# A hybrid decoder layer on one core: one of seven activation tiles moved by 448 bytes within the partition

## The chip, the cores and the metric

The kernel runs on one core of a Trainium2 chip. The time is that of the device for one execution, in microseconds (us). The profile is one execution taken by the hardware profiler; its rows give times in us from the first instruction of the span.

## What is computed

One decoder layer for 512 positions of width 2048, in float32: a combined input projection, eight heads of block-sparse attention beside a Mamba-2 scan, an output projection, and a convolutional gated feed-forward. The change concerns the feed-forward, whose two large products are most of the work of the second half:

```
h = rms_norm(x, norm2_w)
u = causal_dwconv(h @ w_up, ffn_conv_w, ffn_conv_b)      # 2048 -> 2 x 5632
u_gate, u_val = jnp.split(u, 2, axis=-1)
return x + (jax.nn.silu(u_gate) * u_val) @ w_down        # 5632 -> 2048
```

## The kernel before

**Parts.** Ahead of the feed-forward, the projections and the attention's products run through `acc_tile` and `sm_tile` (their instructions stand under line L183, the line of a helper that records them). The feed-forward, from `start_up` and `step_slot` on, is a list of products (`items`) that is run in the order in which it is written; no scheduler changes it.

**High and low parts.** [...]

**Seven products.** The feed-forward's matrix products are made by a Strassen-like scheme: 2 x 2 blocks with seven products P1 to P7 instead of eight. Each product has a fixed kind of activations, which is a combination of blocks, held in a tile of its own: P5 uses `cmb0`, P7 `cmb1`, P1 `cmb2`, P6 `cmb3`, P2 `cmb4`, P3 `cmb5` (K22) and P4 `cmb6` (KT4). A group is one block column of the weights with its seven products. There are 44 groups of the up-projection with eight chunks of 128 rows, and 24 of the down-projection in three passes, with seven, eight and seven chunks. A product of eight chunks is 24 matmuls of 128 x 256, one of seven chunks 21. In the running order the groups are laced: P5 of a group, P3 of the group before, P1, P4 of the group before, P6, P2, P7. In a row of the profile all products but P2 write a tile `x`, and P2 writes `y`; the activation tiles all read `cmb`, so a product is told by its place in the order.

```
    for gi in range(len(groups) + 1):
        for d, x in ((0, "P5"), (1, "P3"), (0, "P1"), (1, "P4"), (0, "P6"), (0, "P2"), (0, "P7")):
            put(gi - d, x)
```

The matmuls of a product are these (`h`, `l` the weights' parts, stationary; `bk` the tile of the kind, moving):

```
                pe.matmul(out, w, bk[:, 0, q, :], start=fresh and q == 0, stop=False, skip_group_check=True)
                pe.matmul(out, w, bk[:, 1, q, :], start=False, stop=False, skip_group_check=True)
            for q in part:
                pe.matmul(out, l[:, q * 128:(q + 1) * 128], bk[:, 0, q, :], start=False, stop=q == n - 1,
```

In chunk q the moving operand starts 1,024 bytes times q into its half of the tile, and the stationary one 512 bytes times q into its tile; both steps are whole numbers of 512, so the difference of their places by 512 is the same in every chunk.

**Places.** A tile takes the same bytes in each of the 128 partitions. The pool `lp` (left side, named `w2`) holds the weights' tiles and `cmb5` and `cmb6`, which are made in `x_split` for the up-projection and in `b_split` for the down passes; the pool `cmb` on the right side holds `cmb0` to `cmb4`. At the left end lies a scratch for DMA descriptors, 16,384 bytes, and everything of the left side stands behind it. The built program of before, and that of the change, have these places (first byte in the partition, and that number's rest by 512):

```
tile                          before                      rest  after                       rest
descriptor scratch            0 to 16383                        0 to 1023
hi2 (three buffers)           55840, 59936, 64032           32  40480, 44576, 48672           32
lo2 (two buffers)             68128, 72224                  32  52768, 56864                  32
cmb5 (P3)                     76320                         32  60960                         32
space                         -                                 77344 to 77791
cmb6 (P4)                     92704                         32  77792                        480
cmb0 (P5), cmb1 (P7)          147424, 163808               480  147424, 163808               480
cmb2 (P1), cmb3 (P6)          180192, 196576               480  180192, 196576               480
cmb4 (P2)                     212960                       480  212960                       480
earlier: A0..A15, B0..B15     46624 to 112159               32  31264 to 96799                32
earlier: hi (three buffers)   33952, 36064, 38176  160,224,288  18592, 20704, 22816  160,224,288
earlier: lo (three buffers)   40288, 42400, 44512  352,416,480  24928, 27040, 29152  352,416,480
attention: PTh, PTl           180192, 184288               480  180192, 184288               480
attention: vh, vl             188384, 192480               480  188384, 192480               480
```

**Order around the change.** TensorE's matmuls wait for ScalarE's `hi2` and VectorE's `lo2`, and the reuse of their results for VectorE and ScalarE, which add the products up. At the beginning of each down pass VectorE and ScalarE also split the seven kinds of the next pass (`b_split`, L1096 and L1097). Loads are issued by the queue of SyncE (SP).

Of the kernel before, what the change touches and what calls it, by code (L numbers as in the profile page):

```python
# [20 lines left out]
F32 = mybir.dt.float32  # L21
# [166 lines left out]
def body(ctx, tc, xT, wi, wz, wo, wu, wd0, wd1, wd2, pp, pf, outT, dbg={}):  # L188
    nc = tc.nc
# [672 lines left out]
    def cmb_tile(t):  # L862

        pool = p2["cmb"] if t < K22 else p2["cmbl"]
        return pool.tile([128, 2, 8, 256], F32R, name="cmb%d" % t)
# [104 lines left out]
    lp = ctx.enter_context(tc.tile_pool(name="w2", bufs=1, reuse_waits="tile"))  # L970
# [150 lines left out]
    def x_load(n):  # L1121
        if n < 4:
            x_ld.append(side_tile(box["pool"], [4, 256], "ld", 3))
            sy.dma_start(x_ld[n], xd[:, 4 * (n % 2):4 * (n % 2) + 4, n // 2, :])

    def x_split(n):
        t, h = (K22, KT4)[n // 2], n % 2
        if h == 0:
            up_kinds[t] = cmb_tile(t)
        o = up_kinds[t][:, :, 4 * h:4 * h + 4, :]  # L1130
        se.activation(o[:, 0], x_ld[n], AF.Copy)
        ve.tensor_tensor(o[:, 1], x_ld[n], o[:, 0].bitcast(F32), op=OP.subtract)
        x_load(n + 3)

    for n, slot in enumerate((2, 4, 5, 6)):
        at(slot, x_split, n)
# [135 lines left out]
    for k, (gi, x) in enumerate(items):  # L1272
# [8 lines left out]
        n = g["n"]  # L1281
# [36 lines left out]
```

## Time and profile before

| | us |
|---|---|
| three runs | 2113.61, 2114.42 (median), 2114.91 |
| the profiled execution's own time | 2114.84 |
| its span, first to last instruction | 2113.1 |
| TensorE busy in matmuls | 2073.9 |
| VectorE busy | 1583.5 |
| ScalarE busy | 988.3 |
| GpSimd busy | 207.9 |

The profiled execution lies 0.42 us above the median of the runs and 0.07 below the highest; 1.7 us of it lie outside the span. PE is TensorE, DVE VectorE, ACT ScalarE, POOL GpSimd, and PEld the loading of weights. Matmuls are pipelined, so the length of one in a row (0.28 us) is longer than the distance from its start to the next one's start; it is the starts that tell the pace.

### The profile page before, as it was taken

The numbers are of one execution on the slowest core, as the hardware profiler recorded it, in microseconds if no ns is written. First come the engines' busy times: TensorE is split into PE (matmuls) and PEld (weight loads), VectorE is DVE, ScalarE is ACT, GpSimd is POOL, SyncE is SP. The second block draws the span as 40 slices with busy tenths as digits, with TensorE's granted clock in tenths as the row PEclk, the third lists the DMA queues.
The fourth block names the chain that finished last, engine by engine and source line by source line (L and its number), as shares of the span: only waits on it lengthen the run. The fifth ranks groups of instructions, "written<-read, shape, count | busy, mean of one in ns | idle before, by whom it ended". The sixth has DMA issues, their size and how long they took to land.

```text
span 2113.1 us, 37694 instructions
## 1 busy us (share of the span) xinstructions
PE 2073.9 (98%) x15366; PEld 1949.7 (92%) x15366; DVE 1583.5 (75%) x2251; ACT 988.3 (47%) x1433; POOL 207.9 (10%) x107
## 2 busy tenths in 40 slices
PE   9999999999999998999999999999999899999999
PEld 7888887888888878999999999999999899899999
DVE  6545555345555558999999999999999977977976
ACT  5433435244344435555555555555555534534532
POOL 0020000000000001111110111011111111101110
PEclk9999999999999999999999999999999999999999
DMA  5233222332225535445444444454455667856763
GB/s 194 75 115 91 71 75 76 99 101 80 80 70 172 165 129 188 158 141 189 160 156 165 170 168 155 157 183 158 142 188 201 215 215 242 274 184 231 260 201 120
DMA packets 114396, 328.18 MB, mean 155 GB/s; under 512 B 10736, under 2 KB 35120, under 8 KB 111408
## 3 DMA queue, kind: packets, MB, share of 16 engines
q1 hardware_dynamic: 114224, 325.78, 45.5%
q8 instruction: 120, 1.97, 0.4%
q14 instruction: 52, 0.43, 0.1%
HBM read 283.77 MB, written 41.98 MB: 154 GB/s over the span
## 4 chain that ended last, share of the span: by engine, by line
PE 88%; DVE 7%; issue 2%; ACT 1%; DMA 1%; SPq 0%; DVEq 0%; POOL 0%; ACTq 0%; POOLq 0%
PE acc L183 29%; PE x L1289 16%; PE x L1286 16%; PE x L1287 16%; PE sm L183 4%; PE y L1289 3%; PE y L1287 3%; PE y L1286 3%; DVE lo L1050 2%; DVE cmb L1097 1%; DVE lo L183 1%; DVE acc L1151 0%; DVE s L1024 0%; DMA raw<-wi 0%; DVE s L1030 0%
## 5 line engine op out<-in xcount | busy, mean ns | idle before, releaser
L1287 PE MATMUL x<-cmb,hi 128*128 128x256 f32 x3168 | 755.0, 279 | 12.5 <-DVE cmb L1097 10.9
L1286 PE MATMUL x<-cmb,hi 128*128 128x256 f32 x3168 | 755.8, 279 | 11.5 <-ACT cP L1166 5.4
L1287 PEld LDWEIGHTS x<-cmb,hi 128*128 128x128 f32 x3168 | 599.3, 189 | 15.2 <-DVE cmb L1097 13.4
L1286 PEld LDWEIGHTS x<-cmb,hi 128*128 128x128 f32 x3168 | 598.7, 189 | 13.4 <-issue 7.5
L1289 PE MATMUL x<-cmb,lo 128*128 128x256 f32 x3168 | 434.3, 279 | 2.6 <-DVE lo L1050 2.6
L1289 PEld LDWEIGHTS x<-cmb,lo 128*128 128x128 f32 x3168 | 397.2, 189 | 3.6 <-DVE lo L1050 3.4
L183 DVE TENSOR_TENSOR lo<-raw,hi 128x512 fp32r<-128x512 f32 (+1 forms) x240 | 164.4, 691 | 243.0 <-ACT hi L183 228.5
L1041 ACT ACTIVATE hi<-s 128x1024 fp32r<-128x1024 f32 (+1 forms) x201 | 201.0, 1000 | 287.3 <-DVE s L1024 192.2
L1017 POOL TENSOR_TENSOR rawb<-rawa,rawb 128x1024 f32<-128x1024 f32 (+1 forms) x68 | 169.7, 2496 | 1308.1 <-DVE s L1024 1070.8
L183 PE MATMUL acc<-A,hi 128*128 128x512 f32 x704 | 281.5, 400 | 0.5 <-ACT hi L183 0.5
L183 PE MATMUL acc<-A,lo 128*128 128x512 f32 x704 | 277.9, 395 | 0.1
L183 PE MATMUL acc<-B,hi 128*128 128x512 f32 x704 | 276.8, 393 | 0.0
L183 ACT ACTIVATE hi<-raw 128x512 fp32r<-128x512 f32 (+1 forms) x240 | 149.6, 629 | 256.2 <-PE acc L183 220.3
L1050 DVE TENSOR_TENSOR lo<-s,hi 128x1024 fp32r<-128x1024 f32 (+1 forms) x201 | 238.6, 1187 | 18.8 <-issue 18.8
L1050 DVE TENSOR_TENSOR lo<-rawa,hi 128x1024 fp32r<-128x1024 f32 (+1 forms) x204 | 242.0, 1186 | 3.6 <-PE x L1289 3.6
L1041 ACT ACTIVATE hi<-rawa 128x1024 fp32r<-128x1024 f32 (+1 forms) x204 | 209.5, 1028 | 40.0 <-PE x L1287 39.9
L183 PEld LDWEIGHTS acc<-A,lo 128*128 128x128 f32 x704 | 132.1, 188 | 33.0 <-DVE lo L183 2.1
L183 PEld LDWEIGHTS acc<-A,hi 128*128 128x128 f32 x704 | 132.7, 188 | 29.5 <-ACT hi L183 1.8
L183 PEld LDWEIGHTS acc<-B,hi 128*128 128x128 f32 x704 | 132.5, 188 | 28.3
L1166 ACT ACTIVATE cP<-x 128x256 f32<-128x256 f32 x132 | 50.9, 385 | 214.0 <-PE x L1289 214.0
L183 PE MATMUL acc<-hi,A 128*128 128x256 f32 (+2 forms) x448 | 135.4, 302 | 0.7 <-DVE u L183 0.7
L183 PE MATMUL acc<-lo,A 128*128 128x256 f32 (+2 forms) x448 | 133.5, 298 | 0.0
(204 smaller groups left out, 2777.2 us busy)
## 6 DMA issues: line engine op xcount, KB each, us to landing
rawa<-wu SPq DMA_DIRECT2D x176, 512.0 KB, 3.6
raw<-wi SPq DMA_DIRECT2D x79, 512.0 KB, 3.6
rawa<-wd SPq DMA_DIRECT2D x64, 448.0 KB, 4.1
rawb<-wu SPq DMA_DIRECT2D x44, 512.0 KB, 4.5
gd<-gt SPq DMA_DIRECT2D x22, 1024.0 KB, 4.6
raw<-wo SPq DMA_DIRECT2D x32, 512.0 KB, 3.6
rawa<-wd SPq DMA_DIRECT2D x32, 512.0 KB, 4.4
ld<-gd SPq DMA_DIRECT2D x27, 512.0 KB, 6.4
```

Source lines behind the costliest of these rows:

```text
L183: return fn(out, *args, **kw)
L1017: po.tensor_tensor(r, raw[gi, "11"][:, :n], r, op=OP.subtract)
L1041: se.activation(h[:, :n], src[:, :n], AF.Copy)
L1050: ve.tensor_tensor(l[:, :n], src[:, :n], h[:, :n].bitcast(F32), op=OP.subtract)
L1097: ve.tensor_tensor(lo, ld[:, :m, :], hi.bitcast(F32), op=OP.subtract)
L1166: se.activation(g[x], X[:, 256:] if x == "P5" else X[:, :256], AF.Copy)
L1286: pe.matmul(out, w, bk[:, 0, q, :], start=fresh and q == 0, stop=False, skip_group_check=True)
L1287: pe.matmul(out, w, bk[:, 1, q, :], start=False, stop=False, skip_group_check=True)
L1289: pe.matmul(out, l[:, q * 128:(q + 1) * 128], bk[:, 0, q, :], start=False, stop=q == n - 1, skip_group_check=True)
```

## The change

A tile of 112 float32 numbers per partition, named `space`, is taken from the left pool between `cmb5` and `cmb6`; nothing reads or writes it. The scratch for DMA descriptors is made with 1,024 bytes instead of 16,384, so all tiles of the left side begin 15,360 bytes (30 times 512) further left; `cmb6` begins 14,912 bytes further left. Tiles of the right side stay. Each engine has the same instructions in the same order with the same waits; only line numbers behind the added lines are higher by 2.

```
@@ def x_split(n):
         t, h = (K22, KT4)[n // 2], n % 2
+        if n == 2:
+            lp.tile([128, 112], F32, name="space")
         if h == 0:
             up_kinds[t] = cmb_tile(t)
@@ def kernel(**inputs):
-    nc = _bacc.Bacc("TRN2", target_bir_lowering=False, num_devices=1)
+    nc = _bacc.Bacc("TRN2", target_bir_lowering=False, num_devices=1, dynamic_dma_scratch_size=1024)
```

## Rows read from the trace of the kernel before

**Rows 1.** The page: the span, busy time of each engine with its share of the span and its instructions, the DMA queues (packets, MB, share of 16 engines), and the shares by engine of the chain that ended last.

```profile
span 2113.1 us, 37694 instructions
...
PE 2073.9 (98%) x15366; PEld 1949.7 (92%) x15366; DVE 1583.5 (75%) x2251; ACT 988.3 (47%) x1433; POOL 207.9 (10%) x107
...
q1 hardware_dynamic: 114224, 325.78, 45.5%
q8 instruction: 120, 1.97, 0.4%
...
PE 88%; DVE 7%; issue 2%; ACT 1%; DMA 1%; SPq 0%; DVEq 0%; POOL 0%; ACTq 0%; POOLq 0%
```

**Rows 2.** Busy time by stretch of the span: from and to, length, busy time of PE, PEld, DVE, ACT and POOL (number of instructions), then the granted clock of TensorE, the busy share of the DMA engines and GB/s.

```profile
0.00:791.31 791.31, 782.68 (x4266) 664.45 (x4267) 415.14 (x795) 340.51 (x640) 36.32 (x38) 1.00 0.34 106
...
825.29:1649.45 824.16, 824.16 (x7154) 824.16 (x7153) 768.69 (x956) 430.53 (x555) 105.28 (x43) 1.00 0.46 165
1649.45:1707.62 58.17, 46.73 (x365) 44.66 (x364) 54.83 (x72) 30.56 (x36) 7.49 (x3) 0.97 0.73 250
1707.62:1801.99 94.37, 94.37 (x821) 94.37 (x820) 73.10 (x97) 37.12 (x41) 12.52 (x6) 1.00 0.70 231
1801.99:1838.08 36.09, 31.66 (x261) 30.35 (x259) 35.60 (x40) 23.34 (x25) 5.82 (x2) 1.00 0.88 301
1838.08:1967.66 129.58, 129.58 (x1128) 129.58 (x1126) 99.00 (x118) 52.26 (x53) 17.17 (x7) 1.00 0.62 211
1967.66:1994.26 26.60, 23.76 (x195) 22.77 (x193) 26.35 (x33) 15.85 (x19) 3.86 (x1) 1.00 0.85 291
1994.26:2100.68 106.42, 106.42 (x927) 106.42 (x925) 80.84 (x107) 39.81 (x44) 12.80 (x6) 1.00 0.53 177
```

**Rows 3.** TensorE's instructions in order of time in one group of the up-projection: start, length of the row, engine, line, operation, output and inputs, shape, how many. The products begin at 1400.49 (P3), 1403.35 (P1), 1406.09 (P4), 1408.95 (P6), 1411.69 (P2) and 1414.41 (P7).

```profile
1400.49 0.28 PE L1286 MATMUL x<-cmb,hi 128*128 128x256 f32 x1
...
1402.39 1.12 PE L1289 MATMUL x<-cmb,lo 128*128 128x256 f32 x8
1403.35 0.29 PE L1286 MATMUL x<-cmb,hi 128*128 128x256 f32 x1
1403.47 0.28 PE L1287 MATMUL x<-cmb,hi 128*128 128x256 f32 x1
1403.60 0.28 PE L1286 MATMUL x<-cmb,hi 128*128 128x256 f32 x1
1403.71 0.28 PE L1287 MATMUL x<-cmb,hi 128*128 128x256 f32 x1
...
1405.19 1.07 PE L1289 MATMUL x<-cmb,lo 128*128 128x256 f32 x8
1406.09 0.28 PE L1286 MATMUL x<-cmb,hi 128*128 128x256 f32 x1
...
1407.99 1.12 PE L1289 MATMUL x<-cmb,lo 128*128 128x256 f32 x8
1408.95 0.29 PE L1286 MATMUL x<-cmb,hi 128*128 128x256 f32 x1
...
1411.69 0.28 PE L1286 MATMUL y<-cmb,hi 128*128 128x256 f32 x1
...
1413.51 1.07 PE L1289 MATMUL y<-cmb,lo 128*128 128x256 f32 x8
1414.41 0.28 PE L1286 MATMUL x<-cmb,hi 128*128 128x256 f32 x1
```

**Rows 4.** The same view: the first matmul of P4 in the second group of the up-projection that runs P4, and in the 43rd, which is 41 groups later (the one before the first of these begins at 825.29).

```profile
844.65 0.28 PE L1286 MATMUL x<-cmb,hi 128*128 128x256 f32 x1
...
1638.41 0.28 PE L1286 MATMUL x<-cmb,hi 128*128 128x256 f32 x1
```

**Rows 5.** The same view in the last pass of the down-projection, seven chunks: the first matmul of P7, P5, P3, P1, P4 and P6.

```profile
1999.04 0.28 PE L1286 MATMUL x<-cmb,hi 128*128 128x256 f32 x1
...
2001.42 0.28 PE L1286 MATMUL x<-cmb,hi 128*128 128x256 f32 x1
...
2003.80 0.28 PE L1286 MATMUL x<-cmb,hi 128*128 128x256 f32 x1
...
2006.30 0.29 PE L1286 MATMUL x<-cmb,hi 128*128 128x256 f32 x1
...
2008.70 0.28 PE L1286 MATMUL x<-cmb,hi 128*128 128x256 f32 x1
...
2011.20 0.29 PE L1286 MATMUL x<-cmb,hi 128*128 128x256 f32 x1
```

**Rows 6.** What TensorE waited for from 1649.45 us to the end: the waiting line and its output, the releaser, us in total, times, the longest.

```profile
PE x L1287 <- DVE cmb L1097: 10.9, 11, 2.3
...
PE y L1287 <- DVE cmb L1097: 2.8, 3, 2.0
```

**Rows 7.** TensorE in order of time before the feed-forward, columns as in rows 3: a run of nine matmuls of attention with `PTh`, `PTl`, `vh` and `vl` and the one behind it, then a piece of a projection with 512 columns (moving A or B, stationary hi or lo).

```profile
268.25 0.28 PE L183 MATMUL sm<-PTh,vh 128*128 128x256 f32 x1
...
269.33 0.28 PE L183 MATMUL sm<-kh,qh 128*128 128x256 f32 x1
...
492.16 0.39 PE L183 MATMUL acc<-A,hi 128*128 128x512 f32 x1
...
493.54 0.39 PE L183 MATMUL acc<-A,hi 128*128 128x512 f32 x1
```

More of the change, by code (lines that the diff above doesn't have):

```diff
@@ L1127, in x_split @@
         t, h = (K22, KT4)[n // 2], n % 2
+        if n == 2:
+            lp.tile([128, 112], F32, name="space")
         if h == 0:
@@ L1306 @@
     from concourse.bass_utils import run_bass_kernel_spmd as _run
-    nc = _bacc.Bacc("TRN2", target_bir_lowering=False, num_devices=1)
+    nc = _bacc.Bacc("TRN2", target_bir_lowering=False, num_devices=1, dynamic_dma_scratch_size=1024)
     arrays = layout(**{k: _np.asarray(v) for k, v in inputs.items()})
```

## The prediction

> **What bounds the kernel now.** I read the head of the page first. TensorE is busy for 98% of the span, VectorE for 75%, and the chain that ended last lies on TensorE for 88% [rows 1]. Such shares are averages, so I cut the span where TensorE begins or ceases to wait [rows 2]. In four stretches its busy time equals the length of the stretch: 825.29 to 1649.45, 1707.62 to 1801.99, 1838.08 to 1967.66 and 1994.26 to 2100.68, together 824.16 + 94.37 + 129.58 + 106.42 = 1154.5 us. All four are made of the products P1 to P7, at a granted clock of 1.00. Between them lie the hand-overs to the next pass, where VectorE is busy nearly throughout (54.83 of 58.17 us, 35.60 of 36.09, 26.35 of 26.60) and TensorE waits, mostly for the split of a kind (L1097) [rows 2, 6]. So in the four stretches a nanosecond taken from a matmul comes off the end, and in the hand-overs it does not.
>
> Then I read the timeline of one group, product by product, since the change touches one product [rows 3]. A product ends where the next begins. P3 runs from 1400.49 to 1403.35, 2.86 us; P1 2.74; P4 2.86; P6 2.74; P2 2.72. Every product is the same 24 matmuls of 128 x 256. The rows of eight low-part matmuls show the pace itself: 1.12 us in P3 and P4, 1.07 in P1 and P2. One matmul is 0.28 long and seven more steps follow, so a step is (1.12 - 0.28)/7 = 0.120 us against (1.07 - 0.28)/7 = 0.113. No wait stands in these rows; the difference is in the matmuls. P3 and P4 stream `cmb5` and `cmb6`, and those are the two kinds whose first byte, counted by 512, is 32 like that of the weights; the other five stand at 480 (the table of places above).
>
> P1 and P6 are 0.02 us longer than P2, and the rows of P1 show where: its first three starts lie 0.12, 0.13 and 0.11 apart, from the fourth on 0.113 to 0.115. They are the two products that follow a slow one, and the slowness reaches a few matmuls into them.
>
> **What the change does, and its price.** The instructions, their order and their waits are the same; only places differ. Two things move.
>
> First, `cmb6` goes from 32 to 480 by 512, the place of the five fast kinds. P4 should then run like P2: 2.72 instead of 2.86, 0.14 us. P6 loses its slow start, 2.74 to 2.72, 0.02 us. That is 0.16 us of a group, whose length is now (1638.41 - 844.65)/41 = 19.36 us [rows 4]. In the down passes of seven chunks P7 and P5, from 1999.04 to 2003.80, take 2.38 each, P3 and P4 2.50, P1 2.40 [rows 5]: there the gain is 0.12 + 0.02 = 0.14. P3 stays slow and so does the start of P1.
>
> How often: there are 44 groups of up and 24 of down, 68 products P4, 52 of eight chunks and 16 of seven. Of them 43 lie in the first full stretch ((1638.41 - 825.29)/19.36 = 42, and one), 6 of seven in the second, 6 of eight in the third and 6 of seven in the fourth. That is 49 x 0.16 + 12 x 0.14 = 9.5 us. The other seven lie in hand-overs and at the end (3 x 0.16 + 4 x 0.14 = 1.0 us); where TensorE waits for VectorE's queue, arriving earlier only lengthens the wait. Bounds are nothing and all of that 1.0; I take 0.2, near nothing, because VectorE is busy for over 94% of each hand-over [rows 2].
>
> Does the faster TensorE run into VectorE? In the long stretch VectorE is busy 768.69 of 824.16 us [rows 2], so idle 55.5 us, 1.3 us a group, and the gain is 0.16. It stays hidden; without that cover, all of the 0.16 would be lost. ScalarE, at 430.53, and the DMA engines, at a share of 0.46 there and 0.70 in the second stretch, have more room.
>
> Second, the smaller scratch moves everything on the left by 15,360 bytes, which is 30 x 512. The distances among left tiles stay, so the 791 us before the products keep their time; distances from left to right tiles change by a multiple of 512. [...] I price this at nothing. The bound on the gain side is nothing too, since the five right-hand kinds already run at the fastest step seen; on the loss side it is the last rival.
>
> Sum: 9.5 + 0.2 = 9.7 us off the profiled execution's 2114.84 (span 2113.1 and 1.7 around it) gives 2105.1. The median of the runs, 2114.42, is 0.4 lower, so the forecast for the median is **2104.7 us**, 0.46% faster.
>
> **The rivals.** *The place, not the offset.* `cmb5` and `cmb6` are also the only two kinds that lie low in the partition, beside the weights; the other five lie above byte 147,000. If two tiles on one side disturb each other whatever their offset, P4 stays at 2.86 and the time at 2114.4. For it: before the products, moving and stationary operands both lie low at offsets that differ by 64 to 480, and the 512-column matmuls from 492.16 to 493.54 take (493.54 - 492.16)/6 = 0.230, or 0.115 for 256 columns, not 0.113 [rows 7]. Against it: attention's `PTh` and `vh` lie high, both at 480, and take (269.33 - 268.25)/9 = 0.120 [rows 7], exactly P4's step. Equal offsets give 0.120 on either side, unequal ones on one side give less. So the offset matters, and the side may matter a little.
>
> [...]
>
> *Half the gain.* If P4 comes to the 0.115 to 0.116 of low tiles at unequal offsets, it takes 24 x 0.1155 = 2.77 us and saves 0.09 a group of eight, 0.08 of seven: 49 x 0.09 + 12 x 0.08 = 5.4 us, 2109.0.
>
> *Slower.* The 15,360 bytes are a whole number of 1,024s, but not of 2,048s. If what counts is the distance by 2,048 or more, the five right-hand kinds get new distances from the weights, 106,944 instead of 91,584 for `cmb0`. A kind that lands badly costs what P4 costs now: 52 x 0.14 + 16 x 0.12 = 9.2 us. One such kind cancels the gain; from two on the kernel is slower, and as all five move alike it would be 5 x 9.2 - 9.7 = 36 us more, 2151. Against it: within a product the weights step by 512 and the activations by 1,024, so the distance passes through every multiple of 512, and P1's starts stay 0.113 to 0.115 apart over all eight chunks: (1405.19 - 1403.71)/13 = 0.114 [rows 3].
>
> **How the numbers follow.** Full gain 0.60, half gain 0.12, no change 0.21, slower 0.07. A change of under 0.2% (4.2 us) is about what a measurement of this kernel cannot tell from none, so faster is 0.60 + 0.12 = 0.72, same 0.21, slower 0.07. The likeliest case alone runs from 2103.4 (all 10.5 us, and 0.5 for the scatter of the runs) to 2106.5 (nothing kept in hand-overs, P4 only at 2.74, and 0.4 for the scatter). With half gain it holds 0.72, so the range must take in no change as well: 2103.4 to 2115.4.
>
> **What the next profile would show.** Right: rows of eight in P4 at 1.07, those of P3 still at 1.12; P4 2.72 and P6 2.72; a group of 19.20; the long stretch 43 x 0.16 = 6.9 us shorter, at 817.3, with VectorE's busy time unchanged; hand-overs as long as before; 791 us ahead of the products. Wrong: P4 still at 1.12 (the place), at 1.08 to 1.10 (half), rows of eight above 1.07 in P1, P2, P5, P6 or P7 (distance by more than 512), or waits of TensorE in the long stretch (VectorE after all).

## The result and the profile after

The changed kernel takes 2104.32 us (median of 4 runs, 2103.83 to 2104.76) where the kernel before, run beside it, takes 2114.66 (4 runs): a ratio of 0.995 with a 95% interval of 0.9932 to 0.9967. The forecast was 2104.7. The page of the profiled execution after, its span and the busy times of the engines, to be read against [rows 1]:

```profile
span 2102.1 us, 37694 instructions
...
PE 2061.9 (98%) x15366; PEld 1938.7 (92%) x15366; DVE 1582.6 (75%) x2251; ACT 988.3 (47%) x1433; POOL 207.9 (10%) x107
```

The span is 11.0 us shorter, and TensorE is busy 12.0 us less with the same 15366 matmuls; the busy times of VectorE, ScalarE and GpSimd are within 1 us of before. The next two views place the 11.0 us. Both give busy time by stretch, columns as in [rows 2]. Each stretch begins with the same product P5 in both kernels, so that lengths can be subtracted. First the kernel before, whose stretch ahead of these is in [rows 2]:

```profile
791.31:816.29 24.98, 17.70 (x132) 16.89 (x133) 17.70 (x24) 9.73 (x16) 6.68 (x3) 0.86 0.64 218
816.29:1649.45 833.16, 832.95 (x7227) 832.75 (x7226) 777.00 (x965) 438.00 (x564) 105.28 (x43) 1.00 0.46 165
1649.45:1717.29 67.84, 56.40 (x449) 54.33 (x448) 62.49 (x82) 33.13 (x39) 9.48 (x4) 0.97 0.71 239
1717.29:1801.99 84.70, 84.70 (x737) 84.70 (x736) 65.44 (x87) 34.55 (x38) 10.53 (x6) 1.00 0.71 238
1801.99:1846.26 44.27, 39.84 (x333) 38.53 (x331) 42.38 (x48) 25.57 (x27) 8.22 (x3) 1.00 0.78 267
1846.26:1962.42 116.16, 116.16 (x1011) 116.16 (x1009) 86.98 (x105) 45.22 (x46) 14.58 (x6) 1.00 0.62 213
1962.42:2001.42 39.00, 36.16 (x303) 35.16 (x301) 37.57 (x47) 22.58 (x26) 6.04 (x3) 1.00 0.78 264
2001.42:2086.12 84.70, 84.70 (x738) 84.70 (x736) 64.36 (x86) 32.34 (x36) 10.67 (x6) 1.00 0.60 199
2086.12:2113.10 26.98, 22.57 (x191) 22.03 (x189) 14.38 (x21) 6.67 (x8) 0.14 (x1) 1.00 0.18 63
```

The changed kernel, from its start:

```profile
0.00:790.29 790.29, 781.78 (x4266) 664.89 (x4267) 415.21 (x795) 340.34 (x640) 36.32 (x38) 1.00 0.33 106
790.29:815.17 24.88, 17.79 (x132) 17.19 (x133) 17.32 (x24) 10.09 (x17) 6.68 (x3) 0.86 0.66 231
815.17:1640.98 825.81, 825.81 (x7227) 825.81 (x7226) 776.29 (x964) 437.61 (x564) 105.07 (x43) 1.00 0.46 166
1640.98:1709.15 68.17, 55.41 (x449) 52.47 (x448) 62.75 (x82) 33.20 (x40) 9.66 (x4) 1.00 0.70 240
1709.15:1793.15 84.00, 84.00 (x737) 84.00 (x736) 65.39 (x87) 34.53 (x38) 10.55 (x6) 1.00 0.71 239
1793.15:1837.33 44.18, 39.76 (x332) 38.45 (x331) 42.38 (x48) 25.72 (x27) 8.19 (x3) 1.00 0.79 270
1837.33:1952.53 115.20, 115.20 (x1010) 115.20 (x1009) 86.98 (x105) 45.23 (x46) 14.56 (x7) 1.00 0.61 214
1952.53:1991.47 38.94, 35.84 (x302) 34.85 (x301) 37.57 (x47) 22.58 (x26) 6.04 (x3) 1.00 0.78 263
1991.47:2075.47 84.00, 84.00 (x737) 84.00 (x736) 64.35 (x86) 32.33 (x36) 10.65 (x6) 1.00 0.59 201
2075.47:2102.10 26.63, 22.34 (x191) 21.80 (x189) 14.39 (x21) 6.67 (x8) 0.14 (x1) 1.00 0.19 63
```

In the stretches in which TensorE never waits the gains are 7.35 (833.16 to 825.81), 0.70, 0.96 and 0.70 us. Of the 7.35, 6.88 are 43 groups by 0.16; the rest, 0.47, lies in one product P1 at the start of the stretch (2.75 us long now, 3.22 before), where TensorE waited 0.2 us for VectorE before and does not wait now. The hand-overs give -0.33, 0.09 and 0.06, and the end 0.35. Ahead of the feed-forward, whose start is at 790.29 instead of 791.31, lie 1.02, and 0.10 in its first waits. Together that is 11.0.

One group of the up-projection after, the rows of eight low-part matmuls of TensorE (those that read `lo`), columns as in [rows 3]. In order they belong to P4, P6, P2, P7, P5, P3 and P1:

```profile
1401.52 1.07 PE L1291 MATMUL x<-cmb,lo 128*128 128x256 f32 x8
1404.23 1.07 PE L1291 MATMUL x<-cmb,lo 128*128 128x256 f32 x8
1406.95 1.07 PE L1291 MATMUL y<-cmb,lo 128*128 128x256 f32 x8
1409.67 1.07 PE L1291 MATMUL x<-cmb,lo 128*128 128x256 f32 x8
1412.39 1.07 PE L1291 MATMUL x<-cmb,lo 128*128 128x256 f32 x8
1415.20 1.12 PE L1291 MATMUL x<-cmb,lo 128*128 128x256 f32 x8
1417.99 1.07 PE L1291 MATMUL x<-cmb,lo 128*128 128x256 f32 x8
```

Only P3 is left at 1.12, which is the pace of 0.120 us a matmul; P4 has come to 1.07, or 0.113. In starts of products: P4 2.720 us (2.861 before), P6 2.720 (2.739), P3 2.861 and P1 2.739 as before, the other three 2.720.

What TensorE waits for from 1640.98 us to the end, columns as in [rows 6]:

```profile
PE x L1289 <- DVE cmb L1097: 11.5, 12, 2.3
PE y L1289 <- DVE cmb L1097: 3.1, 3, 2.1
```

These are the waits of [rows 6], 10.9 and 2.8 us there, 0.9 us longer together: most of what TensorE gains inside a hand-over becomes wait.

### The profile page after: what moved, and what is told of

Same layout as the page of the kernel before. It is cut to its first block, busy times and chain, and to the rows that moved or that the text cites. A ratio compares the mean times of both kernels' runs of the same rounds, so it can differ in the third digit from the quotient of the medians.

```text
span 2102.1 us, 37694 instructions
## 1 busy us (share of the span) xinstructions
PE 2061.9 (98%) x15366; PEld 1938.7 (92%) x15366; DVE 1582.6 (75%) x2251; ACT 988.3 (47%) x1433; POOL 207.9 (10%) x107
## 4 chain that ended last, share of the span: by engine, by line
PE 90%; DVE 6%; DMA 2%; issue 1%; ACT 1%; SPq 0%; DVEq 0%; POOL 0%; ACTq 0%; POOLq 0%
PE acc L183 30%; PE x L1288 16%; PE x L1289 16%; PE x L1291 16%; PE sm L183 4%; PE y L1288 3%; PE y L1289 3%; PE y L1291 3%; DVE lo L1050 1%; DVE cmb L1097 1%; DMA rawa<-wd 1%; DMA ld<-gd 0%; DVE lo L183 0%; DVE acc L1153 0%; DVE s L1024 0%
```

## The experiments

Products below are medians in us over the up-projection, from the start of one product to the start of the next. "Distance" is the place of a kind's tile less that of the weights' tiles, by 512. Each experiment had its own runs of the kernel before beside it, with medians of 2113.2 to 2114.5. The kernels e4, e6, e7, e8 and e12 have one run each, the others four or more. Runs of one kernel lie 1 to 4 us apart (e1_both 11), so for those five the products say more than the time. No kernel leaves out any part of the computation.

| kernel | distance of `cmb5`, `cmb6` | P3 | P1 | P4 | P6 | P2, P7, P5 | us |
|---|---|---|---|---|---|---|---|
| before | 0, 0 | 2.861 | 2.739 | 2.861 | 2.739 | 2.720 | 2114.7 |
| the change | 0, 448 | 2.861 | 2.739 | 2.720 | 2.720 | 2.720 | 2104.3 |
| e5_mirror | 448, 0 | 2.720 | 2.720 | 2.861 | 2.739 | 2.720 | 2104.2 |
| e8_off_192_256 | 192, 256 | 2.720 | 2.720 | 2.861 | 2.739 | 2.720 | 2104.0 |
| e11_off_32_448 | 32, 448 | 2.803 | 2.738 | 2.720 | 2.720 | 2.720 | 2100.2 |
| e6_off_32_480 | 32, 480 | 2.803 | 2.738 | 2.834 | 2.753 | 2.720 | 2113.6 |
| e7_off_64_128 | 64, 128 | 2.830 | 2.727 | 2.849 | 2.827 | 2.826 | 2129.9 |
| e12_off_320_384 | 320, 384 | 2.830 | 2.727 | 2.849 | 2.827 | 2.827 | 2128.0 |
| e1_both | 448, 448 | 2.826 | 2.826 | 2.826 | 2.826 | 2.826 | 2130.7 |
| e4_right_equal | 0, 448; the others 0 | 2.880 | 2.880 | 2.739 | 2.861 | 2.880 | 2150.9 |

**Which part of the change it is.** e2_scratch_only takes the smaller scratch alone, e3_space_only the 448 bytes alone.

```
-    nc = _bacc.Bacc("TRN2", target_bir_lowering=False, num_devices=1)
+    nc = _bacc.Bacc("TRN2", target_bir_lowering=False, num_devices=1, dynamic_dma_scratch_size=1024)
```

> Only the smaller descriptor scratch: everything of the left side moves by 15,360 bytes, cmb6 stays at 32 by 512 like the weights. Offset theory: nothing changes, 2114.5, P3 and P4 at 2.86. If the scratch, or where the left side begins, carried part of the gain: between 2104 and 2114.

2114.11 us (10 runs) beside 2114.16 of the kernel before (13 runs), ratio 1.0 (0.9991 to 1.001).

```
+        if n == 2:
+            lp.tile([128, 112], F32, name="space")
```

> Only the 448 bytes ahead of cmb6, with the scratch of 16 KB as before. Offset theory: the whole gain, 2104.5, P4 and P6 at 2.72. If the scratch matters: above 2105.

2104.13 us, ratio 0.9952 (0.9937 to 0.9967). The whole gain comes from the 448 bytes; of the move of the left side by 15,360 bytes no effect is seen.

**Offset or side.** In e4_right_equal a tile of 448 bytes stands behind `cmb0` to `cmb4` in the right-hand pool, so that these five stand at 32 by 512, like the weights, though on the other side of the partition. `cmb6` is at 480 as in the change.

```
+        p2["cmb"].tile([128, 112], F32, name="space_r")
```

> The change, and 448 bytes at the end of the right-hand pool, so that cmb0 to cmb4 stand at 32 by 512 like the weights, far from them on the other side of the partition; cmb6 stays at 480, cmb5 at 32. If the offset alone counts: P5, P1, P6, P2 and P7 take 2.86 and only P4 is fast at about 2.74 (it follows slow ones); 5 x 9.2 = 46 us more, near 2150. If the place counts (only tiles on one side disturb each other): these five stay at 2.72 and the time near 2104.3.

2150.94 us. Its rows of eight of one group, in the order P3, P1, P4, P6, P2:

```profile
1400.81 1.12 PE L1292 MATMUL x<-cmb,lo 128*128 128x256 f32 x8
1403.69 1.12 PE L1292 MATMUL x<-cmb,lo 128*128 128x256 f32 x8
1406.48 1.07 PE L1292 MATMUL x<-cmb,lo 128*128 128x256 f32 x8
1409.29 1.12 PE L1292 MATMUL x<-cmb,lo 128*128 128x256 f32 x8
1412.17 1.12 PE L1292 MATMUL y<-cmb,lo 128*128 128x256 f32 x8
```

Now P4 is the only fast product (1.07) and all kinds of the right side run at 1.12, as P3 on the left does. Here the offset decides, the side doesn't. The kernel takes 46.6 us longer than the change (2150.94 less 2104.32).

**One kind or the other.** e5_mirror moves `cmb5` to 480 and leaves `cmb6` at 32.

```
-        if n == 2:
-            lp.tile([128, 112], F32, name="space")
+        if h == 0:
+            lp.tile([128, {0: 112, 2: 16}[n]], F32, name="space%d" % n)
```

> The other of the two kinds moved: cmb5 (P3) at 480, cmb6 (P4) at 32 like the weights. With both kinds at 480 the matmuls ran at 0.113 us in some stretches and at 0.118 in others, changing only at waits, and with one equal kind left they fall to 0.113 a few matmuls behind it. If the equal product brings the pace back: P3 and P1 at 2.72, P4 at 2.86, P6 at 2.74, no product at 2.83, 2104.3 as with the change. If it mattered which kind is moved: another time, towards 2130 where the pace locks at 0.118.

2104.2 us, ratio 0.9958 (0.9944 to 0.9972): the same gain, with P3 and P1 fast and P4 and the start of P6 slow.

**Both kinds.** e1_both puts the space ahead of `cmb5`, so that both kinds stand at 480, like the other five.

```
-        if n == 2:
+        if n == 0:
             lp.tile([128, 112], F32, name="space")
```

> The change, and cmb5 (P3) moved by 448 bytes too, so that all seven kinds stand at 480 by 512. If equal offsets of weights and activations are the cause: P3 goes from 2.86 to 2.72 us and P1 loses its slow start (2.74 to 2.72), again about 9.7 us off, near 2094.6; every product of eight chunks 2.72, a group 19.04. If moving one kind had helped for another reason (its distance to cmb5, or its place alone), P3 stays at 2.86 and the time near 2104.3.

The expectation was wrong by 36 us and in its sign: 2130.69 us (2127.95 to 2139.06), ratio 1.0072 (1.0055 to 1.0089), slower than before. The profiled execution is the slowest of the four, 2139.06; how long each pace held in the other three is not shown. TensorE's rows of eight in a hand-over of this kernel, with its waits in the same stretch (columns as in [rows 3] and [rows 6]):

```profile
1838.95 1.10 PE L1291 MATMUL y<-cmb,lo 128*128 128x256 f32 x8
1843.81 1.07 PE L1291 MATMUL x<-cmb,lo 128*128 128x256 f32 x8
1846.53 1.07 PE L1291 MATMUL x<-cmb,lo 128*128 128x256 f32 x8
1850.14 1.07 PE L1291 MATMUL x<-cmb,lo 128*128 128x256 f32 x8
1852.86 1.07 PE L1291 MATMUL x<-cmb,lo 128*128 128x256 f32 x8
1856.48 1.10 PE L1291 MATMUL x<-cmb,lo 128*128 128x256 f32 x8
1859.31 1.10 PE L1291 MATMUL x<-cmb,lo 128*128 128x256 f32 x8
```

```profile
PE x L1289 <- DVE cmb L1097: 2.8, 3, 1.6
PE y L1289 <- DVE cmb L1097: 0.7, 1, 0.7
```

All these matmuls have one and the same distance, and yet they run at two paces: 1.07, which is 0.113 us a matmul, and 1.10, which is (1.10 - 0.28)/7 = 0.117, or 2.826/24 = 0.1178 by products, called 0.118 below. In this stretch the pace changes in products in which TensorE waits, and holds in between. Once, near 1991 us, it changed behind a start that came only 0.03 us late. Where nothing is late it stays: from 819 us to 1667 every product takes 2.826, at a granted clock of 1.00. So a distance of 448 allows 0.113 and does not bring it about. (By 256, which is what counts in e8_off_192_256 and e12_off_320_384 below, 448 is 192.)

**What brings the fast pace back.** The change's own trace has the slower pace too, and loses it. These are rows of eight at the start of its feed-forward, of P7, P3 and P4 (columns as in [rows 3]):

```profile
813.87 1.10 PE L1291 MATMUL x<-cmb,lo 128*128 128x256 f32 x8
819.99 1.12 PE L1291 MATMUL x<-cmb,lo 128*128 128x256 f32 x8
825.51 1.07 PE L1291 MATMUL x<-cmb,lo 128*128 128x256 f32 x8
```

From 809 to 818 us P2, P7 and P5 step at 0.118; behind the first P3, whose places are equal, the pace is 0.113, and so it is again behind the P3 that follows the slow P5 of 1816.55. In e5_mirror the pace stays at 0.118 through P3 and P1 there and turns behind P4, its equal product. e1_both has no equal product, and its pace stays until something comes late. My next theory was that a slow product, one whose places are equal, is enough to bring the fast pace back. e9_brought_back starts from e1_both and makes P3 slow in twelve of the 68 groups, by moving the weights instead of the activations: for these P3 the weights' parts lie 448 bytes further into tiles that are 512 bytes longer.

```
+    BACK = (0, 1, 44, 45, 46, 47, 52, 53, 54, 60, 61, 62)
+    def shift(k):
+        gi, x = items[k]
+        return 112 if x == "P3" and gi in BACK else 0
...
-        h = lp.tile([128, 1024], F32R, name="hi2", bufs=3)
+        h = lp.tile([128, 1152], F32R, name="hi2", bufs=3)[:, shift(k):shift(k) + 1024]
...
-        l = lp.tile([128, 1024], F32R, name="lo2", bufs=2)
+        l = lp.tile([128, 1152], F32R, name="lo2", bufs=2)[:, shift(k):shift(k) + 1024]
```

> Both kinds at 480 by 512 as in the run that took 2130.7, but in 12 of the 68 groups (the first two and those around the hand-overs) the weights of P3 are put 448 bytes further on, so that weights and activations of these P3 stand equal. If the pace can lock at 0.118 behind a wait and an equal product brings it back to 0.113, and then it stays there until the next wait: P3 2.72 in the 56 other groups, every product of the long stretch at 2.72, 56 x 0.16 = 9 us less than the change, near 2095.5. If one kind has to be equal in every group to hold the pace: back to 0.118 soon behind each of them, near 2128.

2138.12 us, ratio 1.0116 (1.0101 to 1.0131). The theory fell, as TensorE's rows of eight around one of the twelve show:

```profile
1866.98 1.07 PE L1297 MATMUL x<-cmb,lo 128*128 128x256 f32 x8
1869.81 1.12 PE L1297 MATMUL x<-cmb,lo 128*128 128x256 f32 x8
1872.65 1.11 PE L1297 MATMUL x<-cmb,lo 128*128 128x256 f32 x8
1875.47 1.10 PE L1297 MATMUL x<-cmb,lo 128*128 128x256 f32 x8
```

The moved P3 runs at 1.12, as equal places do, though the activations stand at 480 here: the difference of the places counts, not the activations' own place. But the pace was fast ahead of it and is 0.118 behind it: here an equal product takes the fast pace away. P1 begins at 0.118 behind all twelve. In the change P5, P3 and P1 stand at 1.07, 1.12 and 1.07. A difference between the two is that there the activations step from 32 to 480 between P3 and P1, and here the weights step; whether that is the reason is not shown.

**Other distances.** Each of these replaces the space by two, with these numbers of float32 ahead of `cmb5` and of `cmb6`: {0: 8, 2: 112} in e6_off_32_480, {0: 16, 2: 16} in e7_off_64_128, {0: 48, 2: 16} in e8_off_192_256, {0: 80, 2: 16} in e12_off_320_384, {0: 8, 2: 104} in e11_off_32_448.

```
+        if h == 0:
+            lp.tile([128, {0: 8, 2: 112}[n]], F32, name="space%d" % n)
```

> cmb5 at 64 by 512 (32 bytes behind the weights' offset), cmb6 at 0 (32 bytes ahead of it). If the cost comes only of equal offsets: P3 and P4 both near 2.72 or, with the pace locked, all near 2.83. If it fades with the distance: P3 and P4 between 2.72 and 2.86.

2113.63 us. The steps within P3 lie between 0.113 and 0.120 by turns (0.117 in the mean, 2.803 in all), those within P4 between 0.115 and 0.123 (0.118, 2.834), so neither distance has one steady pace; behind both, the pace of 0.113 comes back in the up-projection; in the passes of seven chunks it doesn't, and P2, P7 and P5 take 2.473 there, 0.1178 a matmul, instead of 2.380.

> cmb5 64 and cmb6 128 bytes behind the weights' offset by 512. If only equal offsets cost: both near 2.72, or everything at 2.83 for want of a product that brings the pace back. If a range of distances costs, P3 stays near 2.86 while P4 is faster.

2129.9 us. Rows of eight of one group, in the order P5, P3, P1, P4:

```profile
1409.08 1.10 PE L1291 MATMUL x<-cmb,lo 128*128 128x256 f32 x8
1411.91 1.10 PE L1291 MATMUL x<-cmb,lo 128*128 128x256 f32 x8
1414.67 1.07 PE L1291 MATMUL x<-cmb,lo 128*128 128x256 f32 x8
1417.48 1.11 PE L1291 MATMUL x<-cmb,lo 128*128 128x256 f32 x8
```

P1, behind P3 and the step from 64 to 448, is at 1.07; P6, P2, P7 and P5, behind P4 and the step from 128 to 448, stay slow in the long stretch (2.826). So not every step of the activations brings the fast pace back. Nor do the places alone decide it: in the passes of seven chunks the same step from 128 to 448 is followed by 0.113 (P2 at 2.380), the reverse of e6_off_32_480, whose step from 480 to 448 brings 0.113 back with eight chunks and not with seven.

> cmb5 192 and cmb6 256 bytes behind the weights' offset by 512, distances as between A and hi ahead of the feed-forward, where 256 columns took 0.115. If such distances cost something of their own: P3 and P4 at 24 x 0.115 to 0.116, 2.76 to 2.78. If only equality costs: 2.72, or 2.83 with the pace locked.

2103.98 us, product by product the mirror: 192 is as good as 448, and 256 as bad as nothing (2.861). So in this kernel the distance counts by 256.

> cmb5 at a distance of 320, cmb6 at 384. If the distance counts by 256, these are the 64 and 128 of an earlier run and the products repeat it: P3 2.83, P4 2.85, the others 2.83 in the up-projection, the time near 2130. If it counts by 512, 320 and 384 lie on the way from 256 to 448: then something else, P4 nearer 2.72 to 2.80 as it nears 448, and a time below 2120.

2128.04 us, and all seven products of the up-projection within 0.001 us of those at 64 and 128: the period of 256 once more.

> cmb5 stands at 64 by 512, a distance of 32 from the weights; cmb6 at 480, distance 448 as in the change. If each kind has the pace of its own distance, as the run with 32 and 480 suggests (P3 2.803, P1 2.738, the rest at 2.720), a group is 0.06 + 0.00 us shorter than with the change, 52 x 0.06 + 16 x 0.05 = 3.9 us in all: near 2100.4, P3 2.80 and the other six 2.72 to 2.74. If the step from a distance of nothing to 448 is what brings TensorE back to the pace of 0.113, a step from 32 to 448 may not do it: then the products go at 0.118 for whole stretches behind a wait, as with both kinds at 448, and the time is between 2113 and 2131.

2100.19 us (2099.91 to 2100.78), ratio 0.9939 (0.9922 to 0.9955). Its rows of eight for P5, P3 and P1 of one group:

```profile
1410.14 1.07 PE L1291 MATMUL x<-cmb,lo 128*128 128x256 f32 x8
1412.92 1.10 PE L1291 MATMUL x<-cmb,lo 128*128 128x256 f32 x8
1415.68 1.07 PE L1291 MATMUL x<-cmb,lo 128*128 128x256 f32 x8
```

P3 is at 1.10 instead of 1.12, and the step of the activations from a distance of 32 to 448 still brings P1 to 1.07. By products, all 68 of P3, it is 52 x 0.058 + 16 x 0.047 = 3.8 us shorter than the change (P3 2.803 against 2.861, of seven chunks 2.454 against 2.501), of which 3.3 lie in the stretches without waits (49 x 0.058 + 10 x 0.047); its span, 2098.5 us, is 3.6 shorter. It was not timed beside the change; by the medians it lies 4.1 us below it, the shortest of all kernels here, while the intervals of the two ratios overlap; the products are the better evidence.

**The tiles ahead of the feed-forward.** e10_earlier_tiles gives the projections' matmuls a distance of 192 by 256, by starting in `hi` and `lo` 16 or 48 numbers into longer tiles.

```
+    PLACE1 = {False: 16, True: 48}
...
+            z = PLACE1[getattr(pieces[i][3], "tok", False)]
+            h = wpool.tile([128, 640], F32R, name="hi")[:, z:z + 528]
+            l = wpool.tile([128, 640], F32R, name="lo")[:, z:z + 528]
```

> The change, and ahead of the feed-forward hi and lo are placed so that moving minus stationary is 192 by 256 in every matmul of the projections (as 448 is in the fast products), instead of 0 to 192 by turns. If the distance by 256 sets the pace there too: 512 columns at 0.227 instead of 0.231, 256 at 0.113 instead of 0.118, at best 2200 x 0.005 + 1300 x 0.004 = 16 us off the first 791 us, near 2090. If that part locks at the slower pace behind its many waits: 512 columns at 0.235, 5 to 9 us more, near 2112.

2107.01 us (2104.58 to 2107.63), ratio 0.9963 (0.9949 to 0.9977): nothing beyond the change, and in the profile the feed-forward starts at 793.29 instead of 790.29. The projections' matmuls of 256 columns show both paces: 415 of 754 steps are at most 0.115 (115 of 753 in the change), and 323 lie at 0.116 to 0.119, for instance all from 484 to 492 us; the median is 0.114 instead of 0.118. Those of 512 columns, some 2,250, became slower, 0.2333 in the mean instead of 0.2316, which costs more than the others gain. There too the distance allows the fast pace and does not set it.

## Why the prediction was right

*What bounds the kernel* held. TensorE waits nowhere in the four stretches after either, and they carry the gain.

*P4 from 2.86 to 2.72, P6 from 2.74 to 2.72*: measured 2.861 to 2.720 and 2.739 to 2.720, 0.160 us a group; a group of 19.20 was forecast, and (1630.10 - 842.90)/41 = 19.20 is what P4's starts give. In the passes of seven chunks P4 went from 2.501 to 2.380 and P6 from 2.399 to 2.380: 0.14.

*9.5 us in the full stretches* came out at 9.7 (7.35 + 0.70 + 0.96 + 0.70), of which 9.2 are P4 and P6 and 0.47 the wait that vanished at the start; the groups were cut a little differently there. *0.2 in the hand-overs*: -0.2 (-0.33 + 0.09 + 0.06), and 0.35 at the end. The term of nearly nothing was the right one; all of 1.0 was not kept.

*The scratch at nothing*: no row shows which transfers use it, so the price was an estimate; with the smaller scratch alone the kernel takes 2114.11 against 2114.16. *VectorE stays hidden*: busy 1582.6 us, 1583.5 before, and no wait in the long stretch.

*What the sum did not have*: 1.1 us ahead of the products' steady run (1.02 + 0.10). Instructions and waits are the same there, and with the smaller scratch alone the time is that of before; I take it for the scatter of single executions: in the profiles of the kernels whose part ahead is the same, the feed-forward begins between 789.85 and 791.73.

*The rivals.* The place, not the offset, and half the gain: excluded by P4's 2.720 on the left side and by e4_right_equal on the right. Slower by a distance that counts in 2,048: excluded by e2_scratch_only. The 46.6 us that e4_right_equal costs over the change are near the size worked out for five kinds that land badly, 5 x 9.2 = 46.0, but partly by chance: by products a group is 0.80 longer (0.70 with seven chunks), 0.16 a kind instead of 0.14, and only the groups of the stretches without waits pay it, 49 x 0.80 + 10 x 0.70 = 46.2. One reading under the first two rivals was loose: ahead of the feed-forward the offsets differ by 64 to 448, by the table of places, not to 480; by 256 they differ by 0 to 192, and the seven matmuls read there take `hi` and `lo` by turns, so 0.115 is not the pace of one offset.

Two steps gave the right number for a reason that was too narrow, and in the second that was luck. The rest by 512 was taken as what counts; it is the rest by 256. And 0.113 was taken as the pace of five kinds because they stand at 480. e1_both shows that all seven standing there can run at 0.118, and the passage on P1 and P6, "the two products that follow a slow one", priced those as 0.02 us and no more, while behind a slow product the pace of all that followed turned: from 0.118 to 0.113 at the start of the change's feed-forward, from 0.113 to 0.118 in e9_brought_back. The change came out as forecast because it left `cmb5` where it was, as e1_both shows, which differs from it in that place alone; nothing in the prediction weighed this. Had the change moved both, the same working would have forecast 2094.6 and missed by 36 us. That it is the step of the activations in every group that keeps the change fast fits its trace, but is argued and not shown.

Open is what holds the pace, and why it returns behind some steps (0, 32 or 64 to 448 in the up-projection) and not behind others (128 to 448 in e7_off_64_128, and there only with eight chunks). The runs show only when it does.

## What to carry over

Where TensorE is the bound and loads weights for each matmul, as here (15366 of either), read the starts of equal matmuls by tile: here 0.120 us against 0.113 without any wait came from the tiles' places, and a spacer of 448 bytes, without a new instruction, changed it. Try several places, one kind at a time, and time the whole kernel, because here the pace of a product depended on those ahead of it as well (with a distance of 448, 0.113 in the change and 0.1178 in e1_both): moving one kind gave 10 us, moving both cost 16, and the best was a kind at 32 beside one at 448. Look at the pace behind a slow product before pricing its removal.

## What was not expected of the hardware

- The feed-forward's matmuls of 128 x 256, each with a new load of weights, ran at three steady paces at a granted clock of 1.00: 0.120 us where both operands' places are equal by 256 bytes (2.880/24 in e4_right_equal), and where they are 192 apart by 256 (distances 192 and 448) 0.113 (2.720/24 in the change and e8_off_192_256) or 0.1178 (2.826/24 in e1_both). At 32, 128 and 480 the steps vary by turns, 0.117 to 0.119 in the mean (P3 2.803, P4 2.849 and 2.834); at 64 and 320 they are 0.118 (P3 2.830).
- Which of 0.113 and 0.1178 held depended on what happened before: in the profile of e1_both it stayed at 0.1178 for 848 us without a wait and changed where something came late.
- A change of the activations' place from 32 to 480 was followed by 0.113 (P1 behind P3 in the change, 1.07 a row of eight); a change of the weights' place that gave the same two distances was followed by 0.118 (e9_brought_back, 1.11 and 1.10 a row).
